# Fewer gate chunks in attention, earlier loads at the scan, and MLP operands made kind by kind

## The chip, the cores and the metric

The kernel runs on one core of a Trainium2 chip. The metric is the device time of one execution in microseconds (us). A core has five engines that run their own instruction lists side by side: TensorE (PE, matrix products, with PEld for its weight loads), VectorE (DVE), ScalarE (ACT), GpSimd (POOL) and SyncE (SP, which here only starts DMA transfers). ACT starts some transfers too. An engine takes its list in order; an instruction whose input is not there holds up all that stand behind it on that engine.

## The reference

One block of a hybrid encoder on a sequence of 1024 tokens of width 1024, in float32:

```python
h = rms_norm(x, norm1_w[l]) * (1.0 + scale1) + shift1
proj = h @ w_in[l]
q, k, v, xBC, z, dt_raw, gates = jnp.split(proj, offsets, axis=-1)
...
attn = block_attention(q, k, v)                       # 16 heads of 64, 4 kv heads
ssd = ssd_mixer(xBC, z, dt_raw, ...)                  # two-way state-space scan, chunks of 128
g_attn = jax.nn.sigmoid(gates[..., :D_MODEL])
g_ssd = jax.nn.sigmoid(gates[..., D_MODEL:])
merged = g_attn * (attn @ w_attn_out[l]) + g_ssd * (ssd @ w_ssd_out[l])
x = x + gate1 * (merged @ w_o[l])
h2 = rms_norm(x, norm2_w[l]) * (1.0 + scale2) + shift2
ff = jnp.square(jax.nn.relu(h2 @ w_mlp1[l])) @ w_mlp2[l]
x = x + gate2 * ff
```

## The kernel before

**Products.** To keep float32 accuracy each large product is made of three: an operand is split into a high part (a cast to a short format, name ending in h or hi) and a low part (the operand less its high part, l or lo), and high x high, low x high and high x low are added in PSUM. `split` (L167 for the cast, L153 for the subtraction) does that; by default the cast is ACT's and the subtraction DVE's, and `e_hi` and `e_lo` move them to another engine. A chunk of a product with a weight (`gemm_cm`, L205 to L207, PSUM name psg) is 128 columns: two halves of 512 tokens, 8 blocks of depth, 3 matmuls each, 48 matmuls.

**Stages.** By the profile, in us: modulation and w_in's products for the conv, q, k, v and z to 692; attention to 1203, woven with chunks of w_in's gate product; the scan from 1203 to about 1600, woven with two more gate chunks, the eight chunks of w_attn_out and the first six of w_ssd_out; the merge and w_o to 1837; the MLP.

**Attention and the scan.** `weave` takes the steps of two generators in turn by their estimated costs, and within the weave PE's order is the written one (`manual_schedule(engines={PE})`), while the other engines' lists are set by the scheduler's priorities; `high_priority(offset=...)` moves what it encloses ahead. Attention's outputs av are divided by the row sums (`divide`) and written to DRAM tiles av_d on SP's queue; w_attn_out's product reads them back (`load_a`) as 16 tiles araw, which are split into ah and al. The tag araw has three buffers; the tiles ah and al take the 32 slots that the split of h (hh, hl), read by the gate chunks, had. The scan runs backward states first (`bwd_stream`: load xbb, weight it on POOL, one matmul pst, then prevb on DVE, written to pb_d), and then step by step for four groups of eight chunks: loads of xb, bcT, cst, cmv, pbl (a carried backward state, read back from pb_d) and sz; `scan_w` makes the decay matrix from two matmuls psd in two buffers, a masked copy on DVE (COPY_PREDICATED, L1136), an exponential on ACT (L1139) and a product on DVE (w). `load_g` reads the scan's output y as graw, under the same tag as araw, for w_ssd_out.

**From w_o to the MLP.** `x1` is made row tile by row tile (pso, L1406 to L1408) and normalised; its columns are turned on PE (pst, L1391) and modulated on ACT (fa, fb, L1395; the first half's are f0). The MLP's first product is a seven-product scheme on 2 x 2 blocks. Its operands from the second half are T1 = fa - f0, T2 = fb - T1, T3 = fb - fa, T4 = T2 - f0' and B22 = fb, each for four depths j and each split. Before them PE has five pairs of products that need only the first half (`early_ops`, `product`, L1360 to L1362, PSUM name pp, weights wop). `load_raw` (L1503, L1505) loads the weights of a full step as r0 and r1, and `w_sum` adds them on POOL (ws); the first product on T1 needs such a sum.

The lines quoted as L153 are a helper's: every tensor_tensor carries that number, so the names tell them apart.

Of the kernel before, what the change touches and what calls it, by code (L numbers as in the profile page):

```python
# [9 lines left out]
F32 = mybir.dt.float32  # L10
# [8 lines left out]
P = 128  # L19
# [14 lines left out]
QKV_N = 400  # L34
GATES_EARLY = 12
LEAD2 = 0
# [53 lines left out]
def block(ctx: ExitStack, tc: tile.TileContext, ia, out, upto=99, dbg=None):  # L90
# [75 lines left out]
    def split(hi, lo, src, e_hi=None, e_lo=None):  # L166
        (e_hi or A.copy)(hi, src)  # L167
        tt(e_lo or V, lo, src, hi.bitcast(F32), ALU.subtract)
# [707 lines left out]
    with tc.tile_pool(name="p3k", bufs=1, reuse_waits="tile") as p3k, \  # L876
# [11 lines left out]
        def attn_stream():  # L888
# [66 lines left out]
            def divide(b):  # L955
                h, av, hs = b // 2, avs.pop(b), slice((b % 2) * 512, (b % 2 + 1) * 512)
                tt(G, av, av, rzs[h][:, hs], ALU.mult)
                dma(av_d[h // 2][(h % 2) * HD:(h % 2 + 1) * HD, hs], av)

# [75 lines left out]

    def load_g(pool, k0, hi, lo):
        for half in range(2):
            for k in range(KT):
                t = k0 + k
                w = vecT[:, SN + t:SN + t + 1]  # L1040
                r = pool.tile([P, 512], F32, name="graw", tag="araw", bufs=3)
                dma(r, y_d[t // 4][:, t % 4, half * 512:(half + 1) * 512])
                A.activation(hi[k][half], r, AF.Copy, scale=w)
                V.scalar_tensor_tensor(out=lo[k][half], in0=r, scalar=w, in1=hi[k][half].bitcast(F32), op0=ALU.mult, op1=ALU.subtract)

    with tc.tile_pool(name="p4", bufs=1, reuse_waits="tile") as p4, \
            tc.tile_pool(name="ps4", bufs=1, space=PSUM, reuse_waits="tile") as ps4:


# [20 lines left out]
        def bwd_stream(g):  # L1070
            hs = slice(8 * g, 8 * g + 8)
            prev = None
            for c in range(7, 0, -1):
                xb = p4.tile([P, 640], F32, name="xbb", tag="xbb", bufs=4)
                dma(xb, xb_d[g][:, c])
                xt, bt = xb[:, 0:512].rearrange("p (h d) -> p h d", h=8), xb[:, 512:640]
                xd = p4.tile([P, 8, HD], F32, name="xdb", tag="xd", bufs=3)
                tt(G, xd, xt, bc(dec["sb"][:, c, hs].unsqueeze(2), [P, 8, HD]), ALU.mult)
                ps = ps4.tile([P, 512], F32, name="pst", tag="psx", bufs=PSX)
                T.matmul(ps, bt, xd.rearrange("p h d -> p (h d)"), start=True, stop=True)  # L1080
                pb = p4.tile([P, 8, HD], F32, name="prevb", tag="prevb", bufs=2)
                ps3d = ps.rearrange("p (h d) -> p h d", h=8)
                if c == 7:
                    V.tensor_copy(pb, ps3d)
                else:
                    tt(V, pb, prev, bc(dec["cb"][:, c, hs].unsqueeze(2), [P, 8, HD]), ALU.mult)
                    tt(V, pb, pb, ps3d, ALU.add)
                prev = pb
                dma(pb_d[g][c - 1], pb.rearrange("p h d -> p (h d)"))
                yield 1  # L1090
# [103 lines left out]
        def load_a():  # L1194
            for half in range(2):
                ns = slice(half * 512, (half + 1) * 512)
                for k in range(KT):
                    raw = p4.tile([P, 512], F32, name="araw", tag="araw", bufs=3)
                    dma(raw, av_d[k][:, ns])
                    split(ahi[k][half], alo[k][half], raw)  # L1200

# [41 lines left out]
        def products():  # L1243
            yield from gates_stream(p4, ps4, GATES_EARLY, GATES)
            yield from out_stream(ps4, "psg", [w_cols(w_ao, i * P) for i in range(KT)], ahi, alo, a_d, p4, load_a)
            while pipe["done"] < 16:
                yield None
            yield from out_stream(ps4, "psg", [w_cols(w_so, i * P) for i in range(KT - HELD)], ghi, glo, s_d, p4,
                                  lambda: load_g(p4, 0, ghi, glo))

# [127 lines left out]
    with tc.tile_pool(name="p6", bufs=1, reuse_waits="tile") as p6:  # L1378
# [47 lines left out]

        early = [early_ops(p) for p in range(2)]
        early_ps = [[product(early[0][0], B11), product(early[0][1], B21)]]
        mps.close()
# [9 lines left out]
        T1, B22 = act_pairs("t1"), act_pairs("b22")  # L1439
        T2, T3, T4 = hp_pairs("t2"), hp_pairs("t3"), hp_pairs("t4")  # L1440
        for j in range(HK):
            fa, fb = tmp("fa"), tmp("fb")
            modulated(fa, turned(1, j), j)
            modulated(fb, turned(1, HK + j), HK + j)
            t1, t2, t3, t4 = (tmp(f"tt{i}") for i in range(4))
            tt(V, t1, fa, f0[j], ALU.subtract)
            split(*T1[j], t1)
            tt(V, t2, fb, t1, ALU.subtract)
            split(*T2[j], t2, e_lo=G)
            tt(V, t3, fb, fa, ALU.subtract)  # L1450
            split(*T3[j], t3, e_lo=G)
            tt(V, t4, t2, f0[HK + j], ALU.subtract)
            split(*T4[j], t4, e_hi=V.tensor_copy, e_lo=G)
            split(*B22[j], fb, e_hi=V.tensor_copy)
    wos.close()
# [5 lines left out]
    with tc.tile_pool(name="p7", bufs=1, reuse_waits="tile") as p7:  # L1461
# [31 lines left out]
        for p in range(NPRE):  # L1493
            if p:
                if p >= 2:
                    early.append(early_ops(p))
                early_ps.append([product(early[p][0], B11), product(early[p][1], B21)])
            c1s[p] = first_two(p, *early_ps[p])[0]
# [326 lines left out]
```

## Time and profile before

| what | value |
|---|---|
| time, median of 3 runs | 2491.66 us (2490.63 to 2496.14) |
| the profiled execution: its own time | 2494.41 us |
| its span, first to last instruction | 2492.5 us |
| mean granted clock of PE | 0.987 of full speed |
| PE busy | 2406.6 us, 97% of the span |
| DVE, ACT, POOL busy | 1711.5, 1096.5, 852.1 us |

Shares are averages over all stages. What a stage is worth is read from windows: the busy time of each engine in a stretch of the span, with the clock that PE was granted there and the share of time that the 16 DMA engines were busy. A wait is put down to the work that ended last before the waiting instruction. Matmuls overlap, so a row of PE shows a duration longer than the distance to the next.

### The profile page before, as it was taken

How to read it: one execution, taken by the hardware profiler on the slowest of the kernel's cores; microseconds unless marked ns; L12 is line 12 of the kernel's file. 1: busy time of each engine (PE TensorE's matmuls, PEld its weight loads, DVE VectorE, ACT ScalarE, POOL GpSimd, SP SyncE). 2: the span in 40 equal slices, each digit the busy share in tenths (PEclk: the TensorE clock that was granted, in tenths of full speed). 3: DMA queues.
4: the chain of work that ended last, by engine and by line, in shares of the span. 5: the costliest groups of instructions: out<-in, count | busy, mean ns of one | idle time of the engine just before them, and what ended most of it. 6: DMA issues, size and time to landing. Idle time of an engine off the chain costs nothing. (4 is left out here: it accounts for less than half of the span.)

```text
span 2492.5 us, 32192 instructions
## 1 busy us (share of the span) xinstructions
PE 2406.6 (97%) x11307; PEld 1908.9 (77%) x11307; DVE 1711.5 (69%) x2318; ACT 1096.5 (44%) x1882; POOL 852.1 (34%) x650
## 2 busy tenths in 40 slices
PE   8999999999999999999899999998989999999999
PEld 4898877888867777777667767776777888788887
DVE  4756345777756666666577797556569887767794
ACT  5455522555556666666333343344232222364430
POOL 0211107666611111110356666424017866114200
PEclk9999999999999999999999999999999999999999
DMA  7654661333532212111677776466315544554522
GB/s 256 192 166 135 213 205 59 102 102 107 189 107 64 81 52 87 56 58 47 210 208 213 215 223 182 141 229 216 116 51 194 190 148 161 210 191 137 153 81 88
DMA packets 284210, 363.38 MB, mean 146 GB/s; under 512 B 33673, under 2 KB 166513, under 8 KB 284049
## 3 DMA queue, kind: packets, MB, share of 16 engines
q1 hardware_dynamic: 211590, 285.10, 36.8%
q10 hardware_dynamic: 72459, 76.22, 9.1%
q8 instruction: 90, 1.47, 0.3%
q14 instruction: 71, 0.58, 0.1%
HBM read 248.18 MB, written 113.06 MB: 145 GB/s over the span
## 5 line engine op out<-in xcount | busy, mean ns | idle before, releaser
L921 DVE TENSOR_REDUCE nm<-pss 128x1 f32<-128x1024 f32 x128 | 156.7, 1225 | 133.6 <-PE pss L919 132.1
L923 ACT ACTIVATE pf<-pss,nm 128x1024 f32<-128x1024 f32 x128 | 143.1, 1118 | 101.9 <-PE pst L934 99.2
L153 DVE TENSOR_TENSOR pl<-pst,ph 128x512 fp32r<-128x512 f32 x256 | 167.9, 683 | 28.1 <-ACT ph L167 28.1
L934 PEld LDWEIGHTS pst<-masks,pf 128*128 128x128 f32 x1024 | 118.3, 140 | 70.3 <-issue 29.7
L404 PE MATMUL psq<-twh,hh 128*128 128x512 f32 (+1 forms) x448 | 168.9, 380 | 2.3 <-ACT twh L167 1.6
L167 ACT CAST ph<-pst 128x512 fp32r<-128x512 f32 x256 | 146.4, 586 | 54.2 <-PE pst L934 40.9
L405 PE MATMUL psq<-twl,hh 128*128 128x512 f32 (+1 forms) x448 | 168.9, 378 | 0.8 <-DVE twl L153 0.8
L406 PE MATMUL psq<-twh,hl 128*128 128x512 f32 (+1 forms) x448 | 168.8, 378 | 0.0
L934 PE MATMUL pst<-masks,pf 128*128 128x128 f32 x1024 | 157.1, 276 | 11.8 <-DVE pl L153 9.9
L1702 PE MATMUL p<-o,o 128*128 128x512 f32 x400 | 153.6, 390 | 2.5 <-DVE ac L153 1.4
L1703 PE MATMUL p<-o,o 128*128 128x512 f32 x400 | 155.3, 389 | 0.2 <-DVE o L153 0.2
L1704 PE MATMUL p<-o,o 128*128 128x512 f32 x400 | 153.7, 389 | 0.0
L153 POOL TENSOR_TENSOR av<-av,rz 64x512 f32<-64x512 f32 x32 | 41.0, 1282 | 326.8 <-DMA rz<-rz 125.7
L743 DVE SCALAR_TENSOR_TENSOR tap<-pad,cwT,tap 128x1024 f32<-128x1024 f32 x96 | 123.4, 1285 | 5.2 <-ACT tap L741 3.7
L167 ACT CAST wop<-ws 128x512 fp32r<-128x512 f32 x116 | 71.7, 620 | 119.3 <-PE pp L1362 74.1
L153 POOL TENSOR_TENSOR sl<-sl 128x512 f32<-128x512 f32 x32 | 50.1, 1569 | 178.4 <-DVE o L153 72.2
L167 ACT CAST o<-sl 128x512 fp32r<-128x512 f32 x92 | 56.9, 623 | 105.2 <-PE p L1704 88.3
L971 PE MATMUL pv<-pl,v 128*64 128x512 f32 x256 | 102.0, 419 | 0.0
L153 DVE TENSOR_TENSOR o<-sl,o 128x512 fp32r<-128x512 f32 x92 | 72.3, 789 | 40.3 <-ACT o L167 40.2
L167 ACT CAST wop<-r 128x512 fp32r<-128x512 f32 x77 | 47.2, 622 | 113.3 <-DVE ro L1468 44.3
L205 PE MATMUL psg<-hh,whi 128*128 128x512 f32 x224 | 95.3, 425 | 1.4 <-ACT ost L883 1.4
L404 PEld LDWEIGHTS psq<-twh,hh 128*128 128x128 f32 x448 | 84.3, 189 | 14.7 <-ACT twh L167 2.1
(432 smaller groups left out, 7089.5 us busy)
## 6 DMA issues: line engine op xcount, KB each, us to landing
ar<-r SPq DMA_DIRECT2D x100, 256.0 KB
wada<-in_w_ada_dram SPq DMA_DIRECT2D x48, 512.0 KB
r<-in_w_mlp_dram SPq DMA_DIRECT2D x32, 512.0 KB
sl<-in_w_mlp_dram SPq DMA_DIRECT2D x64, 256.0 KB
r<-in_w_in_dram SPq DMA_DIRECT2D x26, 512.0 KB
r<-ro ACTq DMA_DIRECT2D x52, 256.0 KB
r<-as SPq DMA_DIRECT2D x48, 256.0 KB
xb<-cst ACTq DMA_DIRECT2D x20, 512.0 KB
```

The costliest lines, as they stand in the source:

```text
L153: e.tensor_tensor(out=o, in0=a, in1=b, op=op)
L167: (e_hi or A.copy)(hi, src)
L404: T.matmul(o, hhi[k][half][:, sl], hi[:, k % 2, :n], start=k == 0, stop=False)
L405: T.matmul(o, hhi[k][half][:, sl], lo[:, k % 2, :n], start=False, stop=False)
L406: T.matmul(o, hlo[k][half][:, sl], hi[:, k % 2, :n], start=False, stop=k == KT - 1)
L743: V.scalar_tensor_tensor(out=tap, in0=pad[:, k:k + S], scalar=cwT[:, 24 * k + i:24 * k + i + 1], in1=tap, op0=ALU.mult, op1=ALU.add)
L921: V.tensor_reduce(out=nm, in_=ps, axis=AX.X, op=ALU.max, negate=True)
L923: A.activation(pfs[u], ps, AF.Exp, bias=nm, accum_out=zall[:, u:u + 1])
L934: T.transpose(pt[:, k], pf[:, (hf * 4 + k) * P:(hf * 4 + k + 1) * P], ident)
L1702: T.matmul(ps, a[:, 0, sl], b[0], start=start, stop=False)
L1703: T.matmul(ps, a[:, 0, sl], b[1], start=False, stop=False)
L1704: T.matmul(ps, a[:, 1, sl], b[0], start=False, stop=stop)
```

## The change

Three places are changed.

1. `GATES_EARLY` goes from 12 to 11: one gate chunk of 48 matmuls leaves attention and is run at the scan's beginning, so that three stand there and not two.
2. At the scan's beginning the four first xbb tiles and all eight araw tiles of the first half of the tokens are loaded first, at a high priority; araw has eight buffers (graw with it), prevb three. The last head's av is written from ACT's queue.
3. Between w_o and the MLP, fa and fb of all four depths come first; then T1 and T2, T3 and B22, T4 are made kind by kind. All low parts are DVE's (T2, T3 and T4's were POOL's), all high casts ACT's (T4 and B22's were DVE's). t1 and t2 lie in the buffers of x1 (tag x1 of pool p6) and are overwritten by t4's; t3 overwrites fa. The second to fourth early pairs are written between the kinds.

```diff
--- before.py
+++ after.py
@@ -32,7 +32,7 @@
 OFF_K, OFF_V, OFF_X, OFF_B, OFF_C = 1024, 1280, 1536, 3584, 4096
 OFF_Z, OFF_DT, OFF_G = 4608, 6656, 6720
 QKV_N = 400
-GATES_EARLY = 12
+GATES_EARLY = 11
 LEAD2 = 0
 ZEARLY = 2
 DT0, DTS = 12, 5
@@ -955,7 +955,8 @@
             def divide(b):
                 h, av, hs = b // 2, avs.pop(b), slice((b % 2) * 512, (b % 2 + 1) * 512)
                 tt(G, av, av, rzs[h][:, hs], ALU.mult)
-                dma(av_d[h // 2][(h % 2) * HD:(h % 2 + 1) * HD, hs], av)
+
+                (adma if h == NH - 1 else dma)(av_d[h // 2][(h % 2) * HD:(h % 2 + 1) * HD, hs], av)
 
             def values(b, hf):
 
@@ -1033,18 +1034,35 @@
 
         yield from gemm_cm(ps_pool, tag, wsrcs, hi, lo, evac, bufs=bufs, pair=True, then=then)
 
-    def load_g(pool, k0, hi, lo):
+    def load_g(pool, k0, hi, lo, bufs=3):
         for half in range(2):
             for k in range(KT):
                 t = k0 + k
                 w = vecT[:, SN + t:SN + t + 1]
-                r = pool.tile([P, 512], F32, name="graw", tag="araw", bufs=3)
+                r = pool.tile([P, 512], F32, name="graw", tag="araw", bufs=bufs)
                 dma(r, y_d[t // 4][:, t % 4, half * 512:(half + 1) * 512])
                 A.activation(hi[k][half], r, AF.Copy, scale=w)
                 V.scalar_tensor_tensor(out=lo[k][half], in0=r, scalar=w, in1=hi[k][half].bitcast(F32), op0=ALU.mult, op1=ALU.subtract)
 
     with tc.tile_pool(name="p4", bufs=1, reuse_waits="tile") as p4, \
             tc.tile_pool(name="ps4", bufs=1, space=PSUM, reuse_waits="tile") as ps4:
+
+
+        xbb = []
+        with tc.high_priority(offset=LEAD3 + 100):
+            for c in range(7, 3, -1):
+                xbb.append(p4.tile([P, 640], F32, name="xbb", tag="xbb", bufs=4))
+                dma(xbb[-1], xb_d[0][:, c])
+        raws = {}
+
+        def raw_load(i):
+            raws[i] = p4.tile([P, 512], F32, name="araw", tag="araw", bufs=KT)
+            half, k = divmod(i, KT)
+            dma(raws[i], av_d[k][:, half * 512:(half + 1) * 512])
+
+        with tc.high_priority(offset=LEAD3 + 100):
+            for i in range(KT):
+                raw_load(i)
 
 
 
@@ -1071,14 +1089,17 @@
             hs = slice(8 * g, 8 * g + 8)
             prev = None
             for c in range(7, 0, -1):
-                xb = p4.tile([P, 640], F32, name="xbb", tag="xbb", bufs=4)
-                dma(xb, xb_d[g][:, c])
+                if xbb:
+                    xb = xbb.pop(0)
+                else:
+                    xb = p4.tile([P, 640], F32, name="xbb", tag="xbb", bufs=4)
+                    dma(xb, xb_d[g][:, c])
                 xt, bt = xb[:, 0:512].rearrange("p (h d) -> p h d", h=8), xb[:, 512:640]
                 xd = p4.tile([P, 8, HD], F32, name="xdb", tag="xd", bufs=3)
                 tt(G, xd, xt, bc(dec["sb"][:, c, hs].unsqueeze(2), [P, 8, HD]), ALU.mult)
                 ps = ps4.tile([P, 512], F32, name="pst", tag="psx", bufs=PSX)
                 T.matmul(ps, bt, xd.rearrange("p h d -> p (h d)"), start=True, stop=True)
-                pb = p4.tile([P, 8, HD], F32, name="prevb", tag="prevb", bufs=2)
+                pb = p4.tile([P, 8, HD], F32, name="prevb", tag="prevb", bufs=3)
                 ps3d = ps.rearrange("p (h d) -> p h d", h=8)
                 if c == 7:
                     V.tensor_copy(pb, ps3d)
@@ -1193,11 +1214,10 @@
 
         def load_a():
             for half in range(2):
-                ns = slice(half * 512, (half + 1) * 512)
                 for k in range(KT):
-                    raw = p4.tile([P, 512], F32, name="araw", tag="araw", bufs=3)
-                    dma(raw, av_d[k][:, ns])
-                    split(ahi[k][half], alo[k][half], raw)
+                    if half:
+                        raw_load(KT + k)
+                    split(ahi[k][half], alo[k][half], raws[half * KT + k])
 
         ghi, glo = act_tiles("g", KT)
 
@@ -1246,7 +1266,7 @@
             while pipe["done"] < 16:
                 yield None
             yield from out_stream(ps4, "psg", [w_cols(w_so, i * P) for i in range(KT - HELD)], ghi, glo, s_d, p4,
-                                  lambda: load_g(p4, 0, ghi, glo))
+                                  lambda: load_g(p4, 0, ghi, glo, KT))
 
         with tc.manual_schedule(engines=M3):
             weave(tc, (scan(), 32 * (5.54 + YC) + SC0 + 7 * SC1), (products(), 166.4 + (GATES - GATES_EARLY - HELD) * 10.4), lead=LEAD3)
@@ -1424,8 +1444,13 @@
                     modulated(f0[k], ps, k)
                     split(*(B11, B21)[k // HK][k % HK], f0[k], e_hi=V.tensor_copy)
 
-        early = [early_ops(p) for p in range(2)]
-        early_ps = [[product(early[0][0], B11), product(early[0][1], B21)]]
+        early, early_ps = [], []
+
+        def early_pair(p):
+            early.append(early_ops(p))
+            early_ps.append([product(early[p][0], B11), product(early[p][1], B21)])
+
+        early_pair(0)
         mps.close()
         hps = ExitStack()
         hp = hps.enter_context(tc.tile_pool(name="hp", bufs=1, side="right", reuse_waits="tile"))
@@ -1438,20 +1463,43 @@
 
         T1, B22 = act_pairs("t1"), act_pairs("b22")
         T2, T3, T4 = hp_pairs("t2"), hp_pairs("t3"), hp_pairs("t4")
+
+        fa, fb, t1, t2 = {}, {}, {}, {}
         for j in range(HK):
-            fa, fb = tmp("fa"), tmp("fb")
-            modulated(fa, turned(1, j), j)
-            modulated(fb, turned(1, HK + j), HK + j)
-            t1, t2, t3, t4 = (tmp(f"tt{i}") for i in range(4))
-            tt(V, t1, fa, f0[j], ALU.subtract)
-            split(*T1[j], t1)
-            tt(V, t2, fb, t1, ALU.subtract)
-            split(*T2[j], t2, e_lo=G)
-            tt(V, t3, fb, fa, ALU.subtract)
-            split(*T3[j], t3, e_lo=G)
-            tt(V, t4, t2, f0[HK + j], ALU.subtract)
-            split(*T4[j], t4, e_hi=V.tensor_copy, e_lo=G)
-            split(*B22[j], fb, e_hi=V.tensor_copy)
+            fa[j], fb[j] = tmp("fa"), tmp("fb")
+            modulated(fa[j], turned(1, j), j)
+            modulated(fb[j], turned(1, HK + j), HK + j)
+        early_pair(1)
+
+        def lows(*ops):
+            for (h, l), f in ops:
+                tt(V, l, f, h.bitcast(F32), ALU.subtract)
+
+        last = ()
+        for j in range(HK):
+            tj = p6.tile([P, D], F32, name="t12", tag="x1", bufs=5)
+            t1[j], t2[j] = tj[:, 0:512], tj[:, 512:D]
+            tt(V, t1[j], fa[j], f0[j], ALU.subtract)
+            tt(V, t2[j], fb[j], t1[j], ALU.subtract)
+            A.copy(T2[j][0], t2[j])
+            A.copy(T1[j][0], t1[j])
+            lows(*last)
+            last = (T2[j], t2[j]), (T1[j], t1[j])
+        lows(*last)
+        early_pair(2)
+        for j in range(HK):
+            tt(V, fa[j], fb[j], fa[j], ALU.subtract)
+            A.copy(T3[j][0], fa[j])
+            A.copy(B22[j][0], fb[j])
+        for j in range(HK):
+            lows((T3[j], fa[j]))
+        early_pair(3)
+        for j in range(HK):
+            tt(V, t2[j], t2[j], f0[HK + j], ALU.subtract)
+            A.copy(T4[j][0], t2[j])
+            lows((B22[j], fb[j]))
+        for j in range(HK):
+            lows((T4[j], t2[j]))
     wos.close()
     if upto <= 5:
         return dict(x1_d=x1_d)
@@ -1491,10 +1539,8 @@
 
         c1s = {}
         for p in range(NPRE):
-            if p:
-                if p >= 2:
-                    early.append(early_ops(p))
-                early_ps.append([product(early[p][0], B11), product(early[p][1], B21)])
+            if p >= 4:
+                early_pair(p)
             c1s[p] = first_two(p, *early_ps[p])[0]
 
         def load_raw(p):
```

How this moves instructions, at three places.

SP's queue where attention ends and the scan begins (wraw: weights; xbb and xb, bcT, cst, cmv, sz: the scan's operands; araw: attention's outputs). Before:

```order
L1113 DMA sz<-z_102 128x512
L1067 DMA Dbc<-in_ssd_D_dram 128x32
L1199 DMA araw<-av_85 128x512
L1199 DMA araw<-av_86 128x512
L1199 DMA araw<-av_87 128x512
L180 DMA wraw<-in_w_attn_out_dram 128x8x128 x2
L1075 DMA xbb<-xb_94 128x640
L1199 DMA araw<-av_88 128x512
L1089 DMA pb_6_144<-prevb 128x512
L1199 DMA araw<-av_89 128x512
```

and with the change, from the middle of the moved loads on:

```order
L1061 DMA araw<-av_87 128x512
L1055 DMA xbb<-xb_94 128x640
L1061 DMA araw<-av_88 128x512
L1061 DMA araw<-av_89 128x512
L1061 DMA araw<-av_90 128x512
L1061 DMA araw<-av_91 128x512
L1061 DMA araw<-av_92 128x512
L1118 DMA xb<-xb_94 128x640
L1121 DMA bcT<-bc_98 128x2x128
L1127 DMA cst_10839<-cn_168 28x256
L1128 DMA cmv_10843<-cr_166 4x4x256
```

The loads of araw stood behind the scan's first operands, three of them and then one by one between others; now the first eight, with the four first xbb loads between them, stand right behind w_in's last chunk, and the scan's operands follow them.

DVE's list where the MLP's operands are made (tt: temporary; t1 to t4, b22: the operands, h and l their parts; fa, fb: the modulated columns). Before, for one depth:

```order
L153 TENSOR_TENSOR tt_16617<-fa,f_16232 128x512
L153 TENSOR_TENSOR tt_16618<-fb,tt_16617 128x512
L153 TENSOR_TENSOR tt_16619<-fb,fa 128x512
L153 TENSOR_TENSOR t1l_16564<-tt_16617,t1h_16563 128x512
L167 CAST b22h_16571<-fb 128x512
L153 TENSOR_TENSOR tt_16620<-tt_16618,f_16266 128x512
L153 TENSOR_TENSOR tt_16649<-fa,f_16232 128x512
L153 TENSOR_TENSOR b22l_16572<-fb,b22h_16571 128x512
L153 TENSOR_TENSOR wop<-wraw,wop 128x512
L167 CAST t4h_16595<-tt_16620 128x512
```

and with the change, the end of the list and what follows it:

```order
L153 TENSOR_TENSOR t3l_16580<-fa,t3h_16579 128x512
L153 TENSOR_TENSOR t_16690<-t_16690,f_16266 128x512
L153 TENSOR_TENSOR t3l_16582<-fa,t3h_16581 128x512
L153 TENSOR_TENSOR t3l_16584<-fa,t3h_16583 128x512
L153 TENSOR_TENSOR t3l_16586<-fa,t3h_16585 128x512
L153 TENSOR_TENSOR t_16697<-t_16697,f_16283 128x512
L153 TENSOR_TENSOR t_16704<-t_16704,f_16283 128x512
L153 TENSOR_TENSOR t4l_16588<-t_16685,t4h_16587 128x512
L153 TENSOR_TENSOR t4l_16590<-t_16690,t4h_16589 128x512
L153 TENSOR_TENSOR t4l_16592<-t_16697,t4h_16591 128x512
L153 TENSOR_TENSOR t4l_16594<-t_16704,t4h_16593 128x512
L153 TENSOR_TENSOR ro<-c_16821,pp 128x512
```

The casts to b22h and t4h are gone from it, the low parts of t2, t3 and t4 are on it, and all four depths of t4's low parts stand last, ahead of the sums ro of the early pairs.

SP's queue at the MLP's weights (the two r of a step are its two halves, L1503 and L1505, now L1549 and L1551). Before:

```order
L1368 DMA wraw<-in_w_mlp_dram 128x8x128
L1503 DMA r_16897<-in_w_mlp_dram 128x4x256
L1505 DMA r_16899<-in_w_mlp_dram 128x4x256
L1505 DMA r_16903<-in_w_mlp_dram 128x4x256
L1503 DMA r_16901<-in_w_mlp_dram 128x4x256
L1634 DMA b_16905<-r_0_176 128x512
```

and with the change:

```order
L1388 DMA wraw<-in_w_mlp_dram 128x8x128
L1549 DMA r_16885<-in_w_mlp_dram 128x4x256
L1549 DMA r_16889<-in_w_mlp_dram 128x4x256
L1551 DMA r_16887<-in_w_mlp_dram 128x4x256
L1551 DMA r_16891<-in_w_mlp_dram 128x4x256
L1680 DMA b_16893<-r_0_176 128x512
```

The two first-half loads now stand ahead of the two second-half ones.

## The prediction

> **What bounds the kernel now.** I read the engine totals first, then the span cut at the stages, then the two places where TensorE (PE) stands still, through windows, waits and timelines.
>
> ```profile
> PE 2406.6 (97%) x11307; PEld 1908.9 (77%) x11307; DVE 1711.5 (69%) x2318; ACT 1096.5 (44%) x1882; POOL 852.1 (34%) x650
> ...
> 692.00:1203.00 511.00, 497.16 (x2619) 378.00 (x2618) 340.54 (x434) 333.64 (x596) 62.30 (x40) 1.00 0.21 64
> 1203.00:1263.00 60.00, 49.44 (x171) 34.08 (x169) 35.15 (x47) 16.25 (x28) 23.59 (x22) 0.89 0.84 266
> 1263.00:1440.00 177.00, 177.00 (x849) 131.54 (x847) 141.37 (x220) 59.03 (x121) 118.43 (x88) 1.00 0.71 214
> 1440.00:1475.00 35.00, 32.05 (x138) 21.25 (x136) 34.29 (x51) 15.74 (x28) 21.54 (x15) 0.95 0.79 251
> 1837.00:1890.00 53.00, 41.15 (x167) 31.54 (x166) 46.60 (x60) 21.95 (x38) 29.14 (x17) 0.87 0.29 94
> ```
>
> After the window and its length stand the busy times of PE, PEld, DVE, ACT and POOL, then PE's granted clock, the DMA share and GB/s. PE is the bound: 97% of the span, and 177.00 of 177.00 us in the scan's first part. The change leaves the number and kind of PE's instructions alone, so it can only gain where PE waits or runs on a low clock: the beginning of the scan (1203 to 1263: 10.56 us idle) and between w_o and the MLP (1837 to 1890: 11.85 us idle).
>
> The scan's beginning in steps of 5 us, and what PE waited for there (total, times, longest):
>
> ```profile
> 1225.00:1230.00 5.00, 4.83 (x18) 2.93 (x16) 3.69 (x6) 2.15 (x4) 0.00 (x0) 1.00 1.09 322
> 1230.00:1235.00 5.00, 1.56 (x5) 0.77 (x4) 2.26 (x3) 2.69 (x5) 1.71 (x2) 0.92 1.05 403
> 1235.00:1240.00 5.00, 3.83 (x7) 2.01 (x7) 4.90 (x7) 1.11 (x2) 2.47 (x3) 0.50 1.02 343
> 1240.00:1245.00 5.00, 3.45 (x10) 1.88 (x9) 3.29 (x6) 1.72 (x3) 0.96 (x1) 0.84 0.96 350
> 1245.00:1250.00 5.00, 5.00 (x15) 3.33 (x14) 3.51 (x7) 1.97 (x4) 1.05 (x2) 0.71 0.86 263
> 1250.00:1255.00 5.00, 3.39 (x16) 2.46 (x14) 1.09 (x2) 0.94 (x2) 1.04 (x1) 1.00 0.88 263
> 1255.00:1260.00 5.00, 2.38 (x5) 1.36 (x5) 4.37 (x10) 2.32 (x6) 1.05 (x1) 0.81 0.59 183
> 1260.00:1265.00 5.00, 5.00 (x18) 3.46 (x17) 3.96 (x9) 1.83 (x4) 1.95 (x2) 0.85 0.58 184
> ...
> PE psg L205 <- ACT ah L167: 4.3, 3, 2.7
> PE psd L1135 <- DVE psd L1136: 4.1, 1, 4.1
> PE psg L206 <- DVE al L153: 2.0, 4, 1.2
> ```
>
> Idle time is window less PE's busy time: 0.17, 3.44, 1.17, 1.55, 0, 1.61, 2.62 and 0, together 10.56 us. The clock costs about busy time times (1 - clock): 0.12, 1.92, 0.55, 1.45, 0.45 and 0.75, together 5.2 us. This place loses 15.8 us. Why it waits:
>
> ```profile
> 1205.05 1.69 SPq L958 DMA_DIRECT2D av<-av  x2
> ...
> 1220.89 1.38 SPq L1199 DMA_DIRECT2D araw<-av  x3
> ...
> 1225.15 0.62 ACT L167 CAST ah<-araw 128x512 fp32r<-128x512 f32 x1 [10.73 <-DMA araw<-av]
> ...
>   DMA araw<-av: 28.4, 9
> ...
> 1256.75 0.69 DVE L1136 COPY_PREDICATED psd<-below,psd 128x512 f32<-128x512 int32 x1
> ...
> 1205.20 0.39 PE L207 MATMUL psg<-hh,wlo 128*128 128x512 f32 x1
> ...
> 1207.47 0.39 PE L205 MATMUL psg<-hh,whi 128*128 128x512 f32 x1
> ```
>
> Attention's outputs are written at 1205.05, but SP issues the first loads of them at 1220.89, behind the scan's own loads, and only three fit. The first lands for the cast at 1225.15 (4.26 us after issue), the others trickle in (28.4 us of casts waiting), the DMA engines at 0.96 to 1.09. The psd wait is the same lateness: the mask copy stands on DVE behind a late split of araw.
>
> **The change part by part.**
>
> *Chunk moved, loads early.* Ten gate matmuls start in 2.27 us (1205.20 to 1207.47), 0.227 each; the moved chunk of 48 is 10.9 us. It leaves attention and stands between attention's last product and the first product on ah. The twelve loads (four xbb, eight araw, each issue some 0.46 us: 1.38 for three) go right behind w_in's last chunk, the last of them behind the last head's write, which moves to ACT's queue and costs it two issues. By the row at 1205.05 plus 4.3 us, the last of the eight lands near 1206 + 6 + 4.3 = 1216 on the old clock even if nothing runs earlier; the first product on ah then stands at 1229 to 1230, having been wanted at about 1227. What is moved past is SP's cst, cmv, bcT, xb and sz loads, late by 12 x 0.46 = 5.5 us, with about 30 us of matmuls over them. The splits of the first half wait for chunk three's first half to be read (they use its slots) and have its second 24 matmuls, 5.5 us, as cover against eight casts of 0.62. So the 6.3 us of ah and al waits go. What stays is psd: four matmuls for two buffers stand back to back, so the second pair waits for the mask copy and an exponential. The same wait elsewhere:
>
> ```profile
> PE psd L1135 <- DVE psd L1136: 1.6, 2, 1.4
> ```
>
> That is the bound below, 1.4 us; 4.1 is the bound above. I take 2.0, plus the 1.2 us of clock in 1255 to 1265, plus 0.3 for the first carried state, whose load waits in SP's queue behind an xbb load. **Term: 15.8 - 3.5 = -12.3 us**, bounds -7 (psd and its clock stay, and 3 us of split waits) and -15.8.
>
> [...]
>
> *Attention.* Per score block (128) PE has 511/128 = 3.99 us, DVE 2.66, ACT 2.61; without the chunk PE still has 3.91. It stays PE's, so a removed triple shortens its block. **Term 0**; below, 16 blocks that lose a triple losing also 0.25 us of cover: +4; above -2, from its 13.84 us of idle.
>
> *The scan.* One product chunk more runs inside it, one w_so chunk less. DVE gets a gate chunk's low parts, hidden in DVE's 20% of idle time in 1263 to 1440. **Term 0** (-1 to +3). The g loads, now eight buffers deep, come earlier at 1440 to 1475, which loses 2.95 us idle and 1.6 of clock; its PE waits are mostly psd again (the row above): **-0.5** (+2 to -3).
>
> *Operands between w_o and the MLP.*
>
> ```profile
> 1850.00:1860.00 10.00, 5.71 (x34) 4.53 (x33) 10.00 (x11) 5.95 (x10) 6.38 (x5) 0.94 0.00 0
> 1860.00:1870.00 10.00, 8.05 (x24) 6.11 (x23) 10.00 (x12) 3.61 (x6) 5.96 (x4) 0.72 0.00 0
> 1870.00:1880.00 10.00, 8.59 (x37) 6.28 (x36) 10.00 (x18) 5.00 (x9) 6.88 (x3) 1.00 0.68 212
> 1880.00:1890.00 10.00, 5.80 (x15) 3.83 (x14) 9.86 (x8) 2.47 (x4) 9.92 (x7) 0.66 0.53 179
> ...
> PE pp L1360 <- ACT wop L167: 4.2, 2, 3.7
> PE pst L1391 <- ACT fa L1395: 3.7, 1, 3.7
> PE pp L1360 <- ACT fa L1395: 1.9, 1, 1.9
> ...
> 1848.22 0.69 DVE L153 TENSOR_TENSOR tt<-fa,f 128x512 f32<-128x512 f32 x1
> ...
> 1858.40 1.75 DVE L153 TENSOR_TENSOR t1l<-tt,t1h 128x512 fp32r<-128x512 f32 x1
> ...
> 1862.09 0.68 DVE L153 TENSOR_TENSOR tt<-fa,f 128x512 f32<-128x512 f32 x1
> 1862.70 0.68 DVE L153 TENSOR_TENSOR b22l<-fb,b22h 128x512 fp32r<-128x512 f32 x1
> ...
> 1875.21 0.37 SPq L1503 DMA_DIRECT2D r<-in_w_mlp_dram  x1
> ...
> 1880.22 1.71 POOL L153 TENSOR_TENSOR t4l<-tt,t4h 128x512 fp32r<-128x512 f32 x1
> 1881.90 1.70 POOL L153 TENSOR_TENSOR ws<-r,r 128x512 f32<-128x512 f32 x1
> ...
> 1884.31 0.80 PE L1360 MATMUL pp<-t1h,wop 128*128 128x512 f32 x1 [3.74 <-ACT wop L167]
> ```
>
> DVE is full, 10.00 of 10, and PE waits behind it. A subtraction that starts alone takes 0.68 us (0.60 or 0.61 to the next); beside POOL 1.75. POOL's twelve low parts end at 1880.22 + 1.71 = 1881.9, and only then does it add the weights; their cast releases T1's product at 1884.31. After the change those twelve are DVE's, which has 36 subtractions and three weight lows from 1848.2: 39 x 0.60 = 23.4, to 1871.6, against 1876.04 now. The eight high casts that DVE gives up cost ACT 8 x 0.62 = 5 us (a cast's duration at 1225.15), hidden in ACT's 31 us of idle time of 53. The new wait: the second half's weight load (r1) lies on memory of the t1/t2 tiles and waits for the last but one T4 low. It goes out at about 1872, lands 4.3 later (from 1220.89 to 1225.15, an estimate for a load of twice the size: 4.3 to 6) at 1876.5 to 1878; sum 1.3 to 1.7, cast 0.62: T1 at 1879.5. Queued behind r1 on SP are only the MLP's later loads. PE's own early pairs would end near 1871, so its scattered waits become one of about 8 us. **Term: 1879.5 - 1884.31 = -4.8 us**, bounds 0 (r1 eats it) and -10 (T1's start follows PE).
>
> Sum: -12.3 + 0 + 0 - 0.5 - 4.8 = **-17.6 us**. The profiled execution took 2494.41, 2.75 above the median, of which 1.9 lies outside its span; I put the sum on the median: 2491.66 - 17.6 = **2474.1**.
>
> **The rivals.**
>
> A, *pile-up on DVE.* Some 14 splits and 13 state steps, 27 x 0.60 = 16 us, stand on DVE ahead of the first mask copy, and the splits cannot start before chunk three's first half is read. Then psd still waits 4 us and the splits 3: gain 7 there, 2479. For it: DVE was 4.90 of 5 in 1235 to 1240; against: state steps spread over 33 us.
>
> B, *r1 takes POOL's place.* The load lands at 1881, the operands gain nothing: 2478.9. For it: a DMA share of 0.68 there; against: nothing else loads before 1870 (0.00).
>
> C, *every stall goes*: -15.8 and -10 give 2465. Against it: r1's wait and psd's two buffers.
>
> D, *bandwidth.* The loads are only exchanged: the DMA share was already 0.96 to 1.09, so what went late were w_ao's weights instead; half of 15.8 stays: 2478.5.
>
> E, *slower.* Carried states are written, then loaded again by SP behind xbb loads that wait for slots; now graw loads, eight deep, stand in the same queue, and a scan step that gets its state late holds PE. At 28 steps each 0.65 us late the gain is gone; at 1 us the time is 2474 + 28 = 2502. Against it: PE showed no idle time in 1263 to 1440.
>
> That the change does not do what it says (loads still after 1220) is excluded for the loads by their place in SP's queue; it remains only as D.
>
> **How the numbers follow.** Forecast 0.52 (2468 to 2480 by its terms' middles), A 0.17, B 0.09, C 0.08, D 0.07, E 0.07. Two in ten outside leaves out E, half of C's far end and the forecast's worst sum of bounds: 2464 to 2485. Change and no change can be told apart at about 0.2%, 5 us: faster means below 2486.7. All but E lie below it by their middles; giving 0.09 to their upper ends: faster 0.84, same 0.09, slower 0.07.
>
> **What would show it.** Right: the casts to ah wait for no load; PE's ah and al waits are below 1 us together; one psd wait of 1.4 to 2.5; no window at 0.50 there. DVE ends T4's lows by 1872 and no subtraction takes 1.75 until then; POOL's first weight sum starts at 1877 to 1878.5 (less the gain before it) and waits for r1. Attention shorter by 11 us with the same idle time. Wrong: PE idle between 1263 and 1600 on carried states, a mask copy that still waits behind splits, or a weight sum that starts no earlier.

## The result and the profile after

| | before | changed kernel |
|---|---|---|
| median of 6 runs, taken side by side | 2496.22 us (2490.63 to 2498.72) | 2481.93 us (2479.57 to 2484.74) |
| ratio | 1 | 0.9946, interval 0.9933 to 0.9959 |
| the profiled execution, its span | 2494.41, 2492.5 us | 2479.57, 2477.7 us |
| PE's mean granted clock | 0.987 | 0.990 |

The change makes the kernel faster by 0.54%, about 13.5 us. Forecast were 17.6 us and 2474.1; the time lies in the range of 2464 to 2485. The profile of experiment 3 was taken in an execution with a granted clock of 0.845 (2667.32 us) and is used nowhere below.

Engine totals of the changed kernel:

```profile
PE 2395.1 (97%) x11307; PEld 1903.8 (77%) x11307; DVE 1696.7 (68%) x2323; ACT 1098.9 (44%) x1890; POOL 827.1 (33%) x637
```

PE has the same 11307 matmuls. Its busy time still falls by 11.5 us. A matmul counts as busy for longer on a low clock: in the changed kernel's timeline a 512-column product takes 0.63 us at 1243, in a window with a clock of 0.55, and 0.39 at 1225, in one with 1.00. By the mean clocks that is, as an estimate, some 7 us of the 11.5 (0.013 of 2406.6 less 0.010 of 2395.1); the rest is open.

Windows of the changed kernel (window and length, busy times of PE, PEld, DVE, ACT and POOL, PE's granted clock, DMA share, GB/s): attention, the scan's beginning, and the stretch between w_o and the MLP.

```profile
688.00:1189.10 501.10, 486.25 (x2566) 367.81 (x2566) 339.77 (x433) 331.05 (x592) 60.80 (x39) 1.00 0.21 63
...
1220.00:1225.00 5.00, 3.86 (x15) 2.36 (x14) 4.66 (x6) 4.95 (x10) 1.20 (x1) 1.00 1.07 377
1225.00:1230.00 5.00, 5.00 (x22) 3.76 (x21) 5.00 (x7) 0.62 (x1) 3.30 (x3) 1.00 1.03 361
1230.00:1235.00 5.00, 1.93 (x10) 1.26 (x8) 5.00 (x8) 4.17 (x7) 2.48 (x2) 0.93 1.05 399
1235.00:1240.00 5.00, 0.37 (x1) 0.29 (x1) 5.00 (x10) 1.98 (x5) 0.00 (x0) 0.50 0.91 296
1240.00:1245.00 5.00, 5.00 (x12) 3.25 (x12) 4.50 (x9) 1.07 (x3) 2.47 (x2) 0.55 0.62 162
1245.00:1250.00 5.00, 4.61 (x17) 2.84 (x17) 3.37 (x8) 0.60 (x1) 2.09 (x2) 1.00 0.62 205
...
1840.00:1850.00 10.00, 10.00 (x53) 8.28 (x52) 6.75 (x12) 8.12 (x15) 0.00 (x0) 1.00 0.00 1
1850.00:1860.00 10.00, 3.00 (x12) 1.81 (x11) 10.00 (x18) 5.07 (x11) 0.00 (x0) 0.94 0.25 68
1860.00:1870.00 10.00, 6.11 (x16) 4.83 (x17) 9.91 (x17) 4.10 (x8) 1.32 (x1) 0.54 0.52 178
1870.00:1880.00 10.00, 9.40 (x42) 7.33 (x41) 7.98 (x7) 3.20 (x6) 9.84 (x7) 1.00 0.52 174
```

*The scan's beginning.* Idle time is 1.14 + 0 + 3.07 + 4.63 + 0 + 0.39 = 9.2 us, and the clock costs 0.1 + 0.2 + 2.25 = 2.6: the place loses 11.8 us, where it lost 15.8 and 3.5 were expected. The many short stalls have become one hole from 1232 to 1240, with a clock of 0.50 in it and 0.55 behind it. What PE waited for there:

```profile
PE psd L1156 <- DVE psd L1157: 7.7, 1, 7.7
...
PE pst L1101 <- POOL xdb L153: 1.1, 1, 1.1
```

No product waits for ah or al any more. One long wait is left: the second psd pair, for the mask copy on DVE (L1157 here, L1136 before). Its timeline (start, duration, engine, line; in brackets the idle time just before and what ended it):

```profile
1213.08 0.43 SPq L180 DMA_DIRECT2D wraw<-in_w_attn_out_dram  x1
...
1219.26 1.05 ACT L167 CAST whi<-wraw 128x1024 fp32r<-128x1024 f32 x1 [5.56 <-DMA wraw<-in_w_attn_out_dram]
1220.21 4.26 ACT L167 CAST ah<-araw 128x512 fp32r<-128x512 f32 x8
...
1220.34 1.22 DVE L153 TENSOR_TENSOR wlo<-wraw,whi 128x1024 fp32r<-128x1024 f32 x1 [5.68 <-ACT whi L167]
...
1238.29 0.68 DVE L153 TENSOR_TENSOR al<-araw,ah 128x512 fp32r<-128x512 f32 x1
1238.89 0.68 DVE L1157 COPY_PREDICATED psd<-below,psd 128x512 f32<-128x512 int32 x1
...
1239.63 1.42 PE L1156 MATMUL psd<-cmv,cst 128*128 128x512 f32 x2 [7.70 <-DVE psd L1157]
```

DVE is 5.00 of 5 from 1225 to 1240. From 1220.34 to 1238.89 it works off 14 subtractions to al, 8 state steps and 2 of the weights (wlo), and only then comes the mask copy. That list began late: w_attn_out's first weights, issued at 1213.08 behind the loads that were put first and the scan's operands, were cast at 1219.26, and the eight casts to ah stood behind that cast on ACT. DVE had been idle for 5.68 us.

*Between w_o and the MLP.* Idle 7.00 + 3.89 + 0.60 = 11.5 (11.85 before), clock 0.2 + 2.8 = 3.0. The waits of 1837 to 1890 (the same view that showed 4.2, 3.7 and 1.9 us before):

```profile
PE pp L1380 <- ACT c L1534: 8.8, 1, 8.8
...
PE pp L1382 <- DVE wop L153: 2.1, 1, 2.1
...
PE pp L1380 <- ACT wop L167: 0.6, 1, 0.6
```

and its timeline:

```profile
1843.94 1.29 DVE L153 TENSOR_TENSOR t<-fa,f 128x512 f32<-128x512 f32 x2 [2.81 <-PE pst L1411]
...
1862.13 1.22 ACT L1499 CAST t4h<-t 128x512 fp32r<-128x512 f32 x2 [1.79 <-DVE t L153]
1863.26 2.04 ACT L1534 COPY c<-pp 128x512 f32<-128x512 f32 x4
...
1862.62 2.50 DVE L153 TENSOR_TENSOR t4l<-t,t4h 128x512 fp32r<-128x512 f32 x4
...
1864.57 0.92 SPq L1551 DMA_DIRECT2D r<-in_w_mlp_dram  x2
...
1868.68 2.38 POOL L153 TENSOR_TENSOR ws<-r,r 128x512 f32<-128x512 f32 x1 [133.31 <-DMA r<-in_w_mlp_dram]
...
1863.89 0.80 PE L1380 MATMUL pp<-b11h,wop 128*128 128x512 f32 x1 [8.81 <-ACT c L1534]
...
1871.93 0.39 PE L1380 MATMUL pp<-t1h,wop 128*128 128x512 f32 x1
```

DVE's low parts are done at 1865.1, the first T1 product starts at 1871.93 instead of 1884.31. Those two runs reached this stage 10.6 us apart: the last product of w_o (pso) starts at 1826.61 with the change and at 1837.23 before. So the comparison needs distances. Counted from that product, DVE's operand list ends after 38.5 us (38.8 before), r1's loads (L1551) go out after 38.0, and T1 starts after 45.3 (47.1 before): 1.8 us earlier. PE's idle time is nearly what it was. What fell is the time on a low clock: the first ten products behind T1's start took 5.3 us before, with a clock of 0.54 from 1884 to 1890, and 3.2 with the change, with 1.00 from 1870 to 1880.

By the starts of PE's matmuls, from event to event:

| us between PE's starts | before | after | difference |
|---|---|---|---|
| begin of the span to first score product | 692.5 | 688.0 | -4.5 |
| first score product to last product of attention | 509.2 | 501.0 | -8.2 |
| that to the last psd of the scan | 391.8 | 395.3 | +3.5 |
| that to the last product of w_o (pso) | 243.7 | 242.2 | -1.4 |
| that to the end | 650.6 | 646.4 | -4.2 |

The sum is -14.9. Attention and scan belong together, since the chunk goes from one to the other: -4.7 for the part on which -12.8 was forecast (-12.3 and -0.5). The last line is the operands' term: -4.2, against -4.8. The first line is a part in which PE's list is the same but for three gate matmuls, 0.7 us, that leave it.

### The profile page after: what moved, and what is told of

The parts are those of the page before. It is cut to its first block, busy times and chain, and to the rows that moved or that the text cites. A ratio compares the mean times of both kernels' runs of the same rounds, so it can differ in the third digit from the quotient of the medians.

```text
span 2477.7 us, 32208 instructions
## 1 busy us (share of the span) xinstructions
PE 2395.1 (97%) x11307; PEld 1903.8 (77%) x11307; DVE 1696.7 (68%) x2323; ACT 1098.9 (44%) x1890; POOL 827.1 (33%) x637
## 5 line engine op out<-in xcount | busy, mean ns | idle before, releaser
L921 DVE TENSOR_REDUCE nm<-pss 128x1 f32<-128x1024 f32 x128 | 156.7, 1225 | 125.3 <-PE pss L919 122.9
L934 PE MATMUL pst<-masks,pf 128*128 128x128 f32 x1024 | 157.4, 276 | 13.0 <-DVE pl L153 10.6
L153 POOL TENSOR_TENSOR ws<-r,r 128x512 f32<-128x512 f32 x29 | 42.7, 1474 | 212.5 <-DMA r<-in_w_mlp_dram 167.0
L153 DVE TENSOR_TENSOR o<-sl,o 128x512 fp32r<-128x512 f32 x92 | 71.5, 780 | 38.6 <-ACT o L167 38.5
L167 ACT CAST wop<-r 128x512 fp32r<-128x512 f32 x77 | 47.1, 622 | 111.1 <-DVE ro L1516 49.6
```

What stands on the lines that cost most here:

```text
L153: e.tensor_tensor(out=o, in0=a, in1=b, op=op)
L921: V.tensor_reduce(out=nm, in_=ps, axis=AX.X, op=ALU.max, negate=True)
L934: T.transpose(pt[:, k], pf[:, (hf * 4 + k) * P:(hf * 4 + k + 1) * P], ident)
```

## The experiments

All ratios are times over those of the kernel before, run beside it (0.001 is 2.5 us), with the 95% interval.

**1. The scan's part alone** and **2. the operands' part alone.** The first is the changed kernel with the operands' code as it was, the second the kernel before with the new operands' code:

```diff
 # 1: against the changed kernel
-        early, early_ps = [], []
...
-        early_pair(0)
+        early = [early_ops(p) for p in range(2)]
+        early_ps = [[product(early[0][0], B11), product(early[0][1], B21)]]
...
+            split(*T2[j], t2, e_lo=G)
```

> The changed kernel with its third part undone: between w_o and the MLP the operands are made as before. Theory 1 (the operands' part gains nothing, because the wait of 8.8 us for a copy c on ACT took the place of the old waits): as the changed kernel, ratio to the kernel before 0.9945 to 0.996, that is -10 to -14 us. Rival (each part gives what the prediction gave it, in proportion): the scan's part is 12.8 of 17.6, so about -10 us of -13.5, ratio 0.996, and the operands' part alone -4.

> The kernel before with the third part alone. Theory 1: 0 to -2 us, PE shows the wait for the copy c again (about 9 us) at the fifth early pair. Rival: -4 to -5 us.

Measured: 0.9980 [0.9970, 0.9989] for the first, 0.9982 [0.9972, 0.9992] for the second: some 5 and 4.5 us. The scan's part alone:

```profile
PE psd L1156 <- DVE psd L1157: 5.0, 1, 5.0
PE pst L1101 <- POOL xdb L153: 2.8, 1, 2.8
```

The operands' part alone:

```profile
PE pp L1360 <- ACT c L1514: 7.2, 1, 7.2
```

Each part brings its own waits along, so these come from that part. From last pso to the end the second took 647.1 us and the first 650.8 (before 650.6, after 646.4): the operands are worth 3.5 to 4.4 us wherever they are. In attention and scan together the first took 896.8 (before 901.0, after 896.3): -4.2. What follows: the total of the operands' term was about right, the scan's was not.

**3. and 10. The moved chunk alone**, twice; the rows below are of the second.

```diff
 # against the kernel before
-GATES_EARLY = 12
+GATES_EARLY = 11
```

> The kernel before with GATES_EARLY 11 alone: three gate chunks at the scan's beginning, but the loads as before. Theory (the third chunk's 11 us of products are cover enough for the late loads): PE's waits for ah and al fall from 6.3 us to under 2, the wait at psd stays at 4 or more, time -4 to -7 us. Rival (the loads themselves had to move): ah and al waits stay above 4 us, time within 3 us of before.

> GATES_EARLY 11 alone a second time, for a profile of an undisturbed run. Theory: time -4 to -6 us as measured; the ah and al waits are gone or under 2 us and a psd wait of 5 us or more stands in their place, as in the changed kernel. Rival: ah waits stay above 4 us and the gain came from elsewhere.

Measured: 0.9979 [0.9970, 0.9989] and 0.9972 [0.9962, 0.9982]. PE's waits at the scan's beginning with the chunk alone, the whole list:

```profile
PE psd L1135 <- DVE psd L1136: 7.6, 1, 7.6
```

The ah and al waits are gone without any earlier load: the chunk gives the late loads the time that they need. What is late then is DVE's list, this time because the casts wait for the loads (17.0 us in 9 waits); the copy comes at 1237.07.

**9. The early loads alone**, with 12 chunks and the old operands:

```diff
 # against the kernel before: the loads of xbb and araw ahead, as in the change
+        with tc.high_priority(offset=LEAD3 + 100):
+            for i in range(KT):
+                raw_load(i)
```

> The kernel before with the early loads alone (second part of the change), GATES_EARLY at 12 and the old operands' part. Two gate chunks are left as cover; the first psd pair stands some 50 matmuls behind the first product on ah, 7 in the changed kernel. Theory (the loads were the lateness, and the third chunk only moved it to VectorE's list): ah and al waits fall below 2 us in all, the psd wait below 3, time -5 to -9 us against before, as much as or more than loads and chunk together (-5, ratio 0.998). Rival (the chunk is what counts: chunk alone measured -5, the same as chunk and loads): time within 3 us of before, ah waits of 3 us or more stay because two chunks cover too little.

Measured: 0.9972 [0.9961, 0.9983]. PE's waits at the scan's beginning with the loads alone:

```profile
PE psg L205 <- ACT whi L167: 7.3, 1, 7.3
...
PE psd L1156 <- DVE psd L1157: 0.8, 1, 0.8
```

The timeline of the same kernel, SP's queue and PE:

```profile
1234.45 1.29 SPq L180 DMA_DIRECT2D wraw<-in_w_attn_out_dram  x2
...
1242.13 0.79 PE L205 MATMUL psg<-ah,whi 128*128 128x512 f32 x1 [7.35 <-ACT whi L167]
```

Its windows there:

```profile
1235.00:1240.00 5.00, 0.00 (x0) 0.00 (x0) 5.00 (x7) 3.15 (x6) 2.94 (x2) 0.78 1.08 379
1240.00:1245.00 5.00, 2.83 (x6) 1.82 (x7) 3.23 (x5) 1.11 (x2) 0.66 (x1) 0.50 1.09 365
```

Now it is w_attn_out's weights that are late, their load issued at 1234.45 behind the others (1222.31 before). So the chunk alone gives -6.2 us in attention and scan, the loads alone -5.9, and both together -3.6 to -5.5 in the seven profiles that have both with the scan unaltered (the changed kernel twice, and experiments 1, 6, 7, 8 and 11): they remove the same stall, and do not add.

**4. The scan's steps later, by the planner's cost** and **5. by a gap of 14 us.** Both let PE do more products ahead of the first psd, so that DVE has time.

```diff
 # 4
-SC0, SC1 = 26, 3.5
+SC0, SC1 = 44, 3.5
 # 5
             for _ in bwd_stream(0):
                 yield SC1
+            yield 14.0
```

> The changed kernel with the scan's assumed cost of beginning at 44 and not 26, so that the weave puts the first psd some 50 matmuls behind the first product on ah and not 7. Theory (the 7.7 us at the first psd are VectorE's list of splits and carried states standing ahead of the mask copy, to 1239 us): the wait falls below 3 us and the time by 5 to 8 us against the changed kernel, ratio to before 0.9915 to 0.993. Rival (the list itself is bound by the loads of the second half and of w_attn_out and moves back with psd): a wait of 6 or more stays, ratio as the changed kernel, 0.9946.

> The changed kernel with the scan's first step 14 us of assumed cost later in the weave, behind the seven backward states, which stay where they are: the first psd pair comes 46 matmuls behind the first product on ah (7 before), with the second pair three products behind the first. Theory (VectorE's list up to the mask copy, over at about 1239 us in the changed kernel, is all that holds psd; the last run moved the backward states too and so left VectorE idle earlier and got a new wait for them): the psd waits fall to under 1.5 us and no wait for xdb over 1.5 appears, PE's loss there from 9.6 us idle to under 4, time -4 to -7 us against the changed kernel, ratio to before 0.992 to 0.9935. Rival (bandwidth: DMA share 1.03 to 1.07 there, the wait turns up at pbl or xbb instead): ratio 0.9945 or more.

Measured: 0.9952 [0.9937, 0.9967] and 0.9963 [0.9948, 0.9977], no faster than the changed kernel (0.9946, and 0.9948 in a later repeat). With the cost at 44 the psd wait shrinks, but the backward states moved too (waits of the scan's beginning):

```profile
PE pst L1101 <- POOL xdb L153: 3.7, 1, 3.7
PE psd L1156 <- DVE psd L1157: 1.4, 1, 1.4
```

With the gap the psd wait is gone at its place, and the weights' split is next (the same view, and the window in which that wait ends):

```profile
PE psg L207 <- DVE wlo L153: 3.0, 1, 3.0
...
PE psd L1156 <- ACT w L1160: 0.5, 1, 0.5
PE psd L1156 <- DVE psd L1157: 0.2, 1, 0.2
```

```profile
1240.00:1245.00 5.00, 4.50 (x13) 3.62 (x14) 2.25 (x4) 0.00 (x0) 0.00 (x0) 0.66 0.86 261
```

To count idle time and slow clock in one, I took each matmul's distance to the next over the usual distance of the same pair. By that measure the scan's beginning loses 17.5 us before, 13.4 after, 8.9 with the cost and 7.3 with the gap: the psd wait was worth what it seemed, there. But with the gap the merge and w_o lose 26.6 instead of 19.3; from 1580 to 1790 PE's waits for split weights with the gap are longer:

```profile
PE pso L1428 <- ACT woh L167: 4.2, 2, 3.5
PE pso L1429 <- DVE wol L153: 3.5, 3, 2.4
PE psg L1363 <- DVE wlo L153: 3.1, 2, 2.6
PE psm L1208 <- POOL u L153: 2.2, 1, 2.2
```

where the changed kernel has 3.2, 3.2, 2.6 and 0.8, and its repeat (12) 3.7, 3.6, 3.8 and 0.8. From the last psd to the last pso the gap's kernel took 239.6 us with 39 matmuls fewer, 8.9 us at 0.227 each; the seven profiles named above took 241.1 to 245.7. So some 3 to 7 us were given back there; single profiles say no more. Why (products taken from the scan's tail, so that less covers what follows it) is argued only. For the cost of 44 the distances from attention to the scan's end are 2 us shorter than after, less than the interval of its time; it stays undecided.

**6., 7. and 8. The operands: r1 free, c early, both.** 6 puts t1 and t2 into other buffers of x1, which was meant to free r1's load of its wait for a T4 low part, and allocates r1 before r0. 7 makes the copy c and the sum of the first pair ahead of T3's casts. 8 does both.

```diff
 # 6
+        for _ in range(3):
+            p6.tile([P, D], F32, name="t12", tag="x1", bufs=5)
 # 7, behind early_pair(2)
+        first_sum()     # A.copy(c1, early_ps[0][0]); tt(V, c, c1, early_ps[0][1], ALU.add)
```

> The changed kernel with the t1/t2 tiles on other buffers of the same pool, so that the first second-half weight load (r1) waits for no T4 low part. Theory (two waits stand side by side: the fifth early pair's wait for the copy c, to 1863.9 us, and the weights, ready at 1871.7; taking one away changes nothing): the weight sum starts 4 us or more earlier, PE still waits 7 to 9 us for c, and the time is within 2 us of the changed kernel. Rival (r1 alone decides): -4 us.

> The changed kernel with the first early pair's copy c and sum made between the operand kinds (in two tiles of their own) and not behind the T4 casts. Theory: PE's wait of 8.8 us for c goes, the fifth pair ends early, and PE then waits as long for the weights that follow r1 (ready at 1871.7): time within 2 us of the changed kernel. Rival (the wait for c is what it costs): -5 to -9 us.

> The two edits before together. Theory: both waits go and VectorE's list is next: T4's low parts end at 1865, then three sums and four squares of the early pairs at 0.60 each, to 1869.3, and T1's first product follows at 1869 to 1869.5 against 1871.9: -2 to -4 us against the changed kernel. Rival (the two waits were all): T1 follows PE at about 1861, -9 us.

Measured: 0.9953 [0.9939, 0.9968], 0.9958 [0.9943, 0.9973], 0.9967 [0.9953, 0.9981]: none faster. In 6 the load came no earlier: it goes out 38.0 us after the last pso, as in the changed kernel, and by the profile it still waits for a T4 low part on DVE. SP's waits in 6 from 1850 to 1872, and its timeline:

```profile
SPq L1551 <- DVE t4l L153: 6.2, 1, 6.2
...
1868.64 0.92 SPq L1551 DMA_DIRECT2D r<-in_w_mlp_dram  x2
```

The changed kernel's SP has the same wait, 6.2 us. So 6 does not test what it was made for. In 7 the wait for c is gone and the weights' wait, which it had hidden, is as long (PE's timeline of 7):

```profile
1873.39 0.79 PE L1380 MATMUL pp<-t1h,wop 128*128 128x512 f32 x1 [9.05 <-ACT wop L167]
```

T1 starts 45.0 us after the last pso, against 45.3: two chains end together, one over DVE's T4 subtractions, ACT's T4 casts and c, the other over DVE's T4 low parts, r1, POOL's sum and ACT's cast. In 8 it is again 45.0: r1 waits for a T4 low part there too, POOL's sum waits for r1, and ACT's cast of it starts at 1871.51, 0.04 us behind the sum's end (POOL's timeline of 8):

```profile
1869.07 2.40 POOL L153 TENSOR_TENSOR ws<-r,r 128x512 f32<-128x512 f32 x1 [132.39 <-DMA r<-in_w_mlp_dram]
```

Whether an r1 that is truly early would shorten the second chain was not reached by any of them and stays open.

**11. The low parts of T2, T3 and T4 on POOL again**, all else as changed.

```diff
-        lows(*last)
+        lows(*last[:1], e=G)
+        lows(*last[1:])
...
-            lows((T4[j], t2[j]))
+            lows((T4[j], t2[j]), e=G)
```

> The changed kernel with the low parts of T2, T3 and T4 on GpSimd again, the order by kinds kept. Theory (the move of the twelve low parts is what frees the place): subtractions of VectorE beside GpSimd take 1.75 us again, GpSimd's twelve end at 1866 or later with the weight sum behind them, time +3 to +6 us against the changed kernel. Rival (the order by kinds is what counts; VectorE is relieved of 12 x 0.60 us): T1 starts at 1872 or earlier, time within 2 us of the changed kernel.

**12. The changed kernel once more**, with no edit, beside 9, 10 and 11.

> The changed kernel itself once more, on the chip of the three runs beside it. If the first ratio holds: 0.9946, -13.5 us; if the parts add up as their own runs say (-5 and -4.5): 0.996, -9.5 us.

Measured: 0.9980 [0.9969, 0.9990] for 11, and 0.9948 [0.9932, 0.9965] for 12, which again waits 7.7 us for psd and 8.8 for c. The move of twelve subtractions from POOL to DVE is worth some 8 us within the change by these times, whose intervals allow 3 to 13, and 5.2 to 5.6 us by the distance from the last pso to the end: the new order with them on POOL needs 652.0 us there, more than the 650.6 before. Timeline of 11:

```profile
1865.89 5.09 DVE L153 TENSOR_TENSOR b22l<-fb,b22h 128x512 fp32r<-128x512 f32 x3
...
1860.32 6.78 POOL L153 TENSOR_TENSOR t3l<-fa,t3h 128x512 fp32r<-128x512 f32 x4
...
1878.15 1.84 POOL L153 TENSOR_TENSOR ws<-r,r 128x512 f32<-128x512 f32 x1 [2.73 <-DMA r<-in_w_mlp_dram]
```

Side by side, from 1860 to 1870, a subtraction took DVE 1.7 us and POOL 1.7 as well, and the weights' sum starts 46.4 us after the last pso, not 42.1. In the changed kernel DVE's stand 0.60 apart from 1844 to 1870 (four t4l in 2.50).

No version was faster than the changed kernel.

## Why the prediction was right, and where not

*The bound.* PE in two places: right. The place and sign of both gains came as forecast: the scan's is in the windows, the operands' in the distances.

*Scan's beginning, -12.3: mis-sized.* The step that failed is "What stays is psd ... I take 2.0". The lines before it held (the loads early, the ah and al waits gone), but psd measured 7.7 and the clock 2.6 us. I took the price of a psd wait from 1440 to 1475. DVE is as full there (34.29 of 35 us, 11 splits of g among it), but those splits stand spread between six mask copies; here 14 stand ahead of one, behind which the cleared stall had piled them up. That is rival A, its 14 splits exact, with 8 state steps and 2 weight splits in place of 13 steps; its start was late because of w_attn_out's weights, which is rival D's sentence, "what went late were w_ao's weights instead" (by their place in the queue; that bandwidth did it is not shown). Experiment 9 shows D's late weights without the late mask copy, 10 the late mask copy without late weights, and the changed kernel has a part of both. Even the bound of -7 was too hopeful: the windows show -4.0.

*Attention, 0.* Attention got 8.2 us shorter, while the 45 matmuls that left it (the other three of the 48 stood ahead of the first score product) are 10.2 us at 0.227 each. Its idle time rose from 13.84 to 14.85. So about 2 us did not come back, within the bound of +4; the profiles with 11 chunks show 500.8 to 501.1, those with 12 show 509.2.

*The scan's inside and gh, 0 and -0.5.* By the measure of experiment 5 the g loads' stretch lost 6.1 us before and 7.0 after: no gain, under 1 us. No step was held by a carried state for more than 1.2 us (rival E did not come).

*Operands, -4.8: the total right, by luck in good part.* It is -4.2 by the distance to the end, 4.5 by experiment 2. But the working's term is T1's start, and that came 1.8 us earlier (1.9 in 12, 1.5 in 2), not 4.8. The step that failed is "39 x 0.60 = 23.4, to 1871.6": it gives DVE no idle time. From the first subtraction, at 1837.57, to the end of the last low part, at 1865.12, DVE took 27.55 us, of which it stood idle 2.81 for the turned columns and 0.79 for a cast of weights. On the clock of the run before, 10.6 us later, r1 then went out at 1875 and not at 1872. The other 2 us or so came behind T1's start, where PE's clock was 1.00 and not 0.54 as before; the working has no term for that. Right were DVE without POOL beside it, the sum that waits for r1, and that the waits become one of about 8 us. Wrong is also what PE waits for in that hole: c, behind T4's casts on ACT, which the working does not have. It cost nothing of its own, because the weights' chain ended at the same time (7 and 8).

The 1.75 us of a subtraction of DVE beside POOL came back in experiment 11 as 1.7, for both engines. Why they slow each other is not shown.

*Clock.* "No window at 0.50" was wrong: 0.50 in 1235 to 1240 and 0.55 behind it, at a wait of 7.7 us. In experiment 5 the window in which a wait of 3.04 us ends (3.43 between the starts of the two matmuls) has 0.66. Before, 0.50 in 1235 to 1240 came behind 3.44 us of idle time in 1230 to 1235, with no ah or al wait over 2.7. How long a wait has to be to bring the clock down is not shown by these rows.

*The sum.* The forecast's terms came to -17.6, those measured in the profile to about -8.9 (-4.7 and -4.2); the time fell by 13.5, with an interval of some 10 to 17. The profiled executions differ by 14.9, of which 4.5 lies ahead of attention, where PE's list is the same but for 0.7 us, and 1.4 in the merge and w_o. The whole range of that first stretch over 13 profiles is 687.7 to 693.2, the changed kernel's two 688.0 and 688.6. Experiments 1, 6, 7, 8 and 11, which share the changed code up to the end of w_o, have 689.9 to 693.2 there, so the chunk and the loads do not set it; whether it is chance is not settled. Nor is it settled why the two parts alone, some 5 and 4.5 us, give less than the 13.5 together; by their intervals that can be chance. So the total was nearer to the forecast than its terms were, and that was luck.

## What to carry to other kernels

A stall has more than one thing late behind it: before pricing its removal, write down for each engine the list that stands ahead of the next instruction PE needs, with its idle time, and take the longest; a wait measured elsewhere had another list ahead of it. Two remedies for one stall (more cover, earlier loads) did not add here (-6.2 and -5.9 us alone, -3.6 to -5.5 together), and the early loads pushed back what shared their queue (w_attn_out's weights went out at 1234.45 in experiment 9, at 1222.31 before). Where two engines slow each other on the same kind of work (side by side a subtraction took DVE 1.70 us and not 0.60, POOL 1.70 and not 1.26), giving all of it to one can be the whole gain, as it was for the operands here (652.0 us with POOL, 646.4 without, 650.6 before). A stall's price is not its idle time alone: the operands' place kept its idle time (11.85 us before, 11.5 after) and still became shorter.

## What the runs showed of the hardware

The beginning of the span, the same in all kernels but for three matmuls (0.7 us), varied by 5.5 us between profiles, so that a single pair of profiles cannot carry a difference of that size. Beside each other, three 128x512 subtractions took DVE 5.09 us and four took POOL 6.78; without POOL, four took DVE 2.50 in the changed kernel, and POOL's last two of experiment 11, begun after DVE's subtractions had ended, took 2.51.
